# One feed-forward pass with its contraction cut into two halves of 64 rows

## The chip, the cores and the metric

The kernel runs on one core of a Trainium2 chip. The metric is the device time of one execution in microseconds (us); lower is better. Engines are named as the profile names them: PE is the matrix engine's matmuls, PEld its weight loads, DVE, ACT and POOL the vector, scalar and general engines, SP the queue that issues the weight DMAs.

## The reference, cut to what matters

The model has two layers: one of gated linear attention and one of stick-breaking attention, each followed by a feed-forward block. The change touches the second layer's feed-forward block, which computes this for 256 tokens, a width of 2048 and 5632 hidden columns, all in float32:

```python
def swiglu(h, w_gate_up, w_down):
    gate, up = jnp.split(h @ w_gate_up, 2, axis=-1)
    return (jax.nn.silu(gate) * up) @ w_down
...
h = h + swiglu(rmsnorm(h, ffn_norm_w[layer]), ffn_w_gate_up[layer], ffn_w_down[layer])
```

## The kernel before, in words

Every weight is read once from HBM, 512 KB at a time. `load_w` (L111) issues one such DMA on SP, then ACT casts the tile `raw` to a rounded tile `hi` (L119), and DVE subtracts to get the rest, `lo` (L120). Activations are kept in the same two parts, so each product is three matmuls: high by high, high by low, low by high. The pool for `hi` and `lo` has three buffers, that for `raw` four. All of these operands have the type float32r.

`gemm_tok` (L123) makes 512 output columns for both tiles of 128 tokens. The contraction of 2048 runs in 16 steps of 128, two steps to a `load_w`. At each step and for each token tile there are three matmuls (L137), with 128x128 activations loaded into the array and 512 weight columns streamed past; all add into one PSUM tile `acc` for each token tile. So one call issues 16 x 2 x 3 = 96 matmuls, each with its own weight load, and a `load_w` feeds 12 of them. At the end `evac` reads `acc`. There are four `acc` banks, so two calls can follow one another without waiting. Two other PSUM pools hold two banks each: `px`, which the attention stages use, and `tr`, for transposes.

`ffn` (L245) goes through the hidden columns in three passes (`PASSES`, of 4, 4 and 3 blocks of 512). For each block of a pass it calls `gemm_tok` for the gate columns, where `evac_gate` runs Silu on ACT from `acc` into `sg` (L258), and then for the up columns, where `evac_up` multiplies on DVE (L261), transposes four 128x128 pieces for each token tile on PE (L264), and splits the result into `hid_h` (ACT, L267) and `hid_l` (DVE, L268). After its blocks, a pass multiplies the hidden columns with the down weights (`residual_gemm`).

```python
                    gemm_tok(w_gu, KD, lhs, b * NB, evac_gate)
                    gemm_tok(w_gu, KD, lhs, DFF + b * NB, evac_up)
```

The order of instructions on each engine is set by the framework's scheduler from a simulated timeline, not strictly by the order of the program text. [...]

`gemm_col` (L157), used elsewhere, alternates matmuls of 512 columns (L169, L172) and of 256 columns (L170), and `level` (L370) has float32 matmuls of 64 columns behind weight loads of 128 columns (L397).

## Time and profile before

| | us |
|---|---|
| median of two runs | 2282.19 (2281.15 to 2283.24) |
| span of the profiled execution, first to last instruction | 2279.7 |
| PE matmul busy | 2263.7 |
| PE weight load busy | 1891.0 |
| DVE busy | 1238.5 |
| ACT busy | 1046.4 |

The profile is of one execution. A busy time is a union of records, and matmul records overlap: a matmul's record runs until its modelled end, while the next one has already begun. The distance from one start to the next tells how fast matmuls follow one another; the length of one record does not.

### The profile page before, as it was taken

To read this page: it belongs to the slowest core of one execution; us is meant where nothing else is said; L and a number is where in the kernel's file an instruction comes from. 1 tells how busy PE (TensorE), PEld (TensorE's weight loads), DVE (VectorE), ACT (ScalarE), POOL (GpSimd) and SP (SyncE) were. 2 spreads that over 40 slices of the span, in tenths; PEclk is the share of its full clock that TensorE was granted. 3 is DMA by queue.
4 is the path that set the end of the run, shared out by engine and by line. 5 is a ranking of instruction groups with operands and counts; after the bars stand their busy time and mean duration, and the time that the engine had idled before them with its cause. 6 is when DMAs were issued, how large, how long until landed. Compare 5 with 4: busy or idle time off the path is not lost.

```text
span 2279.7 us, 27154 instructions
## 1 busy us (share of the span) xinstructions
PE 2263.7 (99%) x10658; PEld 1891.0 (83%) x10658; DVE 1238.5 (54%) x1251; ACT 1046.4 (46%) x1222; POOL 60.4 (3%) x72
## 2 busy tenths in 40 slices
PE   9999999999999999999999999999999999999998
PEld 7888878888888888888888888888888888888887
DVE  6766455545545545544664567655445444554555
ACT  6544444444434443344554446554444344434444
POOL 2100000000000000000000111000000000000000
PEclk9999999999999999999999999999999999999999
DMA  7554555666666666666566654556666666666664
GB/s 224 169 164 143 153 166 181 188 188 190 188 193 193 189 189 193 194 186 193 185 186 194 186 185 141 167 184 191 186 192 190 193 190 192 186 194 193 191 188 157
DMA packets 242712, 419.23 MB, mean 184 GB/s; under 512 B 12972, under 2 KB 64264, under 8 KB 242456
## 3 DMA queue, kind: packets, MB, share of 16 engines
q1 hardware_dynamic: 242408, 416.44, 60.5%
q8 instruction: 83, 1.36, 0.2%
q10 hardware_dynamic: 176, 1.06, 0.1%
q14 instruction: 45, 0.37, 0.0%
HBM read 415.35 MB, written 2.10 MB: 183 GB/s over the span
## 4 chain that ended last, share of the span: by engine, by line
PE 99%; DVE 0%; issue 0%; DMA 0%; ACT 0%; SPq 0%; POOLq 0%; POOL 0%; DVEq 0%; ACTq 0%
PE acc L137 82%; PE acc L169 7%; PE acc L170 4%; PE px L397 1%; PE tr L264 1%; PE tr L194 1%; PE acc L172 0%; PE acc L154 0%; PE px L494 0%; PE tr L525 0%; PE px L439 0%; DMA raw<-in_gla_w_in_dram 0%; DVE B L356 0%; PE px L409 0%; PE tr L526 0%
## 5 line engine op out<-in xcount | busy, mean ns | idle before, releaser
L120 DVE TENSOR_TENSOR lo<-raw,hi 128x1024 fp32r<-128x1024 f32 (+1 forms) x783 | 972.1, 1243 | 938.4 <-ACT hi L119 937.9
L119 ACT CAST hi<-raw 128x1024 fp32r<-128x1024 f32 (+1 forms) x783 | 823.7, 1052 | 1043.1 <-PE acc L137 904.3
L137 PE MATMUL acc<-hi,xhl 128*128 128x512 f32 x4096 | 1274.7, 391 | 0.8 <-ACT xhl L184 0.8
L137 PEld LDWEIGHTS acc<-hi,xhl 128*128 128x128 f32 x4096 | 769.4, 188 | 161.1 <-issue 1.9
L137 PE MATMUL acc<-lo,xhl 128*128 128x512 f32 x2048 | 799.9, 391 | 0.0
L137 PEld LDWEIGHTS acc<-lo,xhl 128*128 128x128 f32 x2048 | 385.1, 188 | 78.7
L137 PE MATMUL acc<-lo,hid_h 128*128 128x512 f32 x680 | 264.9, 390 | 0.0
L137 PE MATMUL acc<-hi,hid_l 128*128 128x512 f32 x680 | 264.6, 389 | 0.0
L169 PE MATMUL acc<-xhl,hi 128*128 128x512 f32 x735 | 256.1, 396 | 0.6 <-ACT hi L119 0.6
L137 PE MATMUL acc<-hi,hid_h 128*128 128x512 f32 x680 | 240.7, 390 | 0.0
L170 PE MATMUL acc<-xhl,lo 128*128 128x256 f32 x784 | 209.6, 281 | 2.1 <-DVE lo L120 2.0
L169 PEld LDWEIGHTS acc<-xhl,hi 128*128 128x128 f32 x735 | 134.8, 188 | 27.7 <-ACT hi L119 1.0
L170 PEld LDWEIGHTS acc<-xhl,lo 128*128 128x128 f32 x784 | 147.7, 189 | 8.8 <-DVE lo L120 3.0
L137 PEld LDWEIGHTS acc<-hi,hid_l 128*128 128x128 f32 x680 | 127.7, 188 | 26.5
L137 PEld LDWEIGHTS acc<-hi,hid_h 128*128 128x128 f32 x680 | 127.6, 188 | 26.3
L137 PEld LDWEIGHTS acc<-lo,hid_h 128*128 128x128 f32 x680 | 127.6, 188 | 26.1
L184 ACT ACTIVATE xhl<-tr,gains 128x256 fp32r<-128x256 f32 x96 | 40.9, 470 | 28.2 <-PE tr L194 20.9
L185 DVE SCALAR_TENSOR_TENSOR xhl<-tr,gains,xhl 128x256 fp32r<-128x256 f32 x96 | 42.4, 478 | 13.0 <-ACT xhl L184 13.0
L235 DVE TENSOR_TENSOR h<-acc,h 128x512 f32<-128x512 f32 x64 | 41.2, 682 | 7.6 <-PE acc L154 5.2
L258 ACT ACTIVATE sg<-acc,n_r 128x512 f32<-128x512 f32 x44 | 30.0, 690 | 20.8 <-PE acc L137 20.8
L267 ACT CAST hid_h<-tr 128x512 fp32r<-128x512 f32 x44 | 23.6, 589 | 31.4 <-PE tr L264 31.4
L268 DVE TENSOR_TENSOR hid_l<-tr,hid_h 128x512 fp32r<-128x512 f32 x44 | 28.3, 686 | 17.3 <-ACT hid_h L267 17.3
(153 smaller groups left out, 709.1 us busy)
## 6 DMA issues: line engine op xcount, KB each, us to landing
raw<-in_ffn_w_gate_up_dram SPq DMA_DIRECT2D x352, 512.0 KB, 3.9
raw<-in_ffn_w_down_dram SPq DMA_DIRECT2D x176, 512.0 KB, 3.7
raw<-in_gla_w_in_dram SPq DMA_DIRECT2D x97, 512.0 KB, 3.9
raw<-in_sb_w_kv_dram SPq DMA_DIRECT2D x64, 512.0 KB, 3.9
raw<-in_gla_w_out_dram SPq DMA_DIRECT2D x32, 512.0 KB, 3.7
raw<-in_sb_w_q_dram SPq DMA_DIRECT2D x32, 512.0 KB, 3.6
raw<-in_sb_w_out_dram SPq DMA_DIRECT2D x32, 512.0 KB, 3.7
h<-in_x_dram SPq DMA_DIRECT2D x8, 256.0 KB, 5.7
```

Of the source, the lines that this page charges most:

```text
L119: a.copy(hi[:, :n], raw[:, :n])
L120: v.tensor_tensor(lo[:, :n], raw[:, :n], hi.bitcast(F32)[:, :n], ALU.subtract)
L137: pe.matmul(acc[t], l, r[:, j, :], start=(k == 0 and n == 0), stop=(k == kt - 1 and n == 2))
L169: pe.matmul(acc[c], hi[:, j, cs], both, start=first, stop=False)
L170: pe.matmul(acc[c][:, :S], lo[:, j, cs], xhl[:, k0 + j, 0, :], start=False, stop=False)
L184: a.mul(dst_h, src, scale)
L185: v.scalar_tensor_tensor(dst_l, src, scale, dst_h.bitcast(F32), ALU.mult, ALU.subtract)
L194: pe.transpose(tp[:, o : o + P], src(t)[:, j * P : (j + 1) * P], ident)
L235: v.tensor_tensor(hs, acc, hs, ALU.add)
L258: a.activation(sg[t], acc, AF.Silu, scale=r[:, t : t + 1])
L267: a.copy(hh[:, :, ts], tv)
L268: v.tensor_tensor(hl[:, :, ts], tv, hh.bitcast(F32)[:, :, ts], ALU.subtract)
```

## The change

Only the first pass of the second layer's feed-forward block is touched: its four blocks with one gate and one up call each, eight calls. They go to a new function, `gemm_rows`. It loads the same weights in the same way, but each matmul over 128 contraction rows becomes two over 64: rows 0 to 63 of the activations and of the weights at array position (0, 0), and rows 64 to 127 at position (64, 0). The halves of one product are issued one behind the other. The first half adds into a bank of `acc`, the second into a bank of `px`. At the end ACT copies the `px` bank into an SBUF tile, DVE adds the `acc` bank to it, and `evac_gate` or `evac_up` reads that sum from SBUF in place of `acc` from PSUM.

```diff
+    def gemm_rows(w_ap, kt, lhs, c0, evac):
+
+        H = P // 2
+        acc = [(ps_acc.tile([P, NB], F32, name="acc"), ps_x.tile([P, 512], F32, name="px")) for _ in range(NT)]
+        for k0 in range(0, kt, 2):
+            hi, lo = load_w(w_ap, k0, 2, c0, NB)
+            for j in (0, 1):
+                k = k0 + j
+                for t in range(NT):
+                    xh, xl = lhs(k, t)
+                    for n, (l, r) in enumerate(((xh, hi), (xh, lo), (xl, hi))):
+                        for half in (0, 1):
+                            rs = slice(half * H, (half + 1) * H)
+                            pe.matmul(acc[t][half], l[rs], r[rs, j, :], start=(k == 0 and n == 0), stop=(k == kt - 1 and n == 2), tile_position=(half * H, 0))
+        for t in range(NT):
+            both = stat.tile([P, NB], F32, name="junk")
+            a.copy(both, acc[t][1])
+            v.tensor_tensor(both, acc[t][0], both, ALU.add)
+            evac(t, both)
...
-                    gemm_tok(w_gu, KD, lhs, b * NB, evac_gate)
-                    gemm_tok(w_gu, KD, lhs, DFF + b * NB, evac_up)
+                    gemm = gemm_rows if layer and blocks is PASSES[0] else gemm_tok
+                    gemm(w_gu, KD, lhs, b * NB, evac_gate)
+                    gemm(w_gu, KD, lhs, DFF + b * NB, evac_up)
```

The rest of the diff takes comments and docstrings out.

## Rows read from the trace of the kernel before

**Rows 1.** The page: the span, busy time by engine (part 1), the granted TensorE clock in 40 slices (part 2, tenths of full speed) and the chain of work that ended last, by engine and by line (part 4).

```profile
span 2279.7 us, 27154 instructions
...
PE 2263.7 (99%) x10658; PEld 1891.0 (83%) x10658; DVE 1238.5 (54%) x1251; ACT 1046.4 (46%) x1222; POOL 60.4 (3%) x72
...
PEclk9999999999999999999999999999999999999999
...
PE 99%; DVE 0%; issue 0%; DMA 0%; ACT 0%; SPq 0%; POOLq 0%; POOL 0%; DVEq 0%; ACTq 0%
PE acc L137 82%; PE acc L169 7%; PE acc L170 4%; PE px L397 1%; PE tr L264 1%; PE tr L194 1%; PE acc L172 0%; PE acc L154 0%; PE px L494 0%; PE tr L525 0%; PE px L439 0%; DMA raw<-in_gla_w_in_dram 0%; DVE B L356 0%; PE px L409 0%; PE tr L526 0%
```

**Rows 2.** Busy time of each engine in stretches of the pass that the change touches, then the granted clock, the DMA engines' share and GB/s: the whole pass's gate and up calls, and the second of its four blocks.

```profile
1542.60:1720.40 177.80, 177.80 (x802) 147.52 (x801) 89.42 (x86) 79.72 (x88) 0.69 (x1) 1.00 0.64 189
...
1587.00:1631.40 44.40, 44.40 (x201) 36.86 (x200) 22.19 (x21) 19.19 (x21) 0.00 (x0) 1.00 0.64 188
```

**Rows 3.** Groups of PE instructions between 1543 and 1721 us: line, operation, output and inputs, shapes, count, busy time, mean ns of one record, idle time before.

```profile
L137 PE MATMUL acc<-hi,xhl 128*128 128x512 f32 x510 | 158.2, 390 | 0.0
L137 PE MATMUL acc<-lo,xhl 128*128 128x512 f32 x256 | 99.7, 390 | 0.0
L264 PE MATMUL tr<-ident,sg 128*128 128x128 f32 x24 | 3.1, 272 | 0.0
```

**Rows 4.** Timeline of PE in the pass, one `load_w` long: start, duration, line, tiles, count merged into the row. Twelve matmuls start from the first row up to the last, the last not counted.

```profile
1709.59 0.39 PE L137 MATMUL acc<-lo,xhl 128*128 128x512 f32 x1
1709.82 0.39 PE L137 MATMUL acc<-hi,xhl 128*128 128x512 f32 x1
1710.04 0.39 PE L137 MATMUL acc<-lo,xhl 128*128 128x512 f32 x1
...
1711.63 0.84 PE L137 MATMUL acc<-hi,xhl 128*128 128x512 f32 x3
1712.31 0.39 PE L137 MATMUL acc<-lo,xhl 128*128 128x512 f32 x1
```

**Rows 5.** Timeline of PEld, the weight loads, at the beginning of the same stretch.

```profile
1709.59 0.19 PEld L137 LDWEIGHTS acc<-hi,xhl 128*128 128x128 f32 x1
1709.82 0.19 PEld L137 LDWEIGHTS acc<-lo,xhl 128*128 128x128 f32 x1
```

**Rows 6.** Timeline of PE in a `gemm_col`, where matmuls of 512 and of 256 columns alternate, each behind a weight load of 128 columns.

```profile
1301.07 0.28 PE L170 MATMUL acc<-xhl,lo 128*128 128x256 f32 x1
1301.19 0.39 PE L169 MATMUL acc<-xhl,hi 128*128 128x512 f32 x1
1301.42 0.28 PE L170 MATMUL acc<-xhl,lo 128*128 128x256 f32 x1
1301.54 0.39 PE L169 MATMUL acc<-xhl,hi 128*128 128x512 f32 x1
...
1303.15 0.28 PE L170 MATMUL acc<-xhl,lo 128*128 128x256 f32 x1
```

**Rows 7.** From the line's own view, the weight loads and matmuls of L397 (count, min/median/max ns); then, from a timeline, a run of 32 of those matmuls of 64 columns.

```profile
L397 PEld LDWEIGHTS px<-lev x224: 187/192/192, 147.8 to 230.0; 128*128 128x128 f32 x112
L397 PE MATMUL px<-lev x224: 217/275/275, 147.9 to 230.1; 128*128 128x64 f32 x112
...
147.91 3.68 PE L397 MATMUL px<-lev 128*128 128x64 f32 x32
```

**Rows 8.** Timelines of ACT and PE around the end of the second block's gate call; a bracket is idle time before and what ended it.

```profile
1606.91 1.05 ACT L119 CAST hi<-raw 128x1024 fp32r<-128x1024 f32 x1 [1.67 <-PE acc L137]
1608.95 1.37 ACT L258 ACTIVATE sg<-acc,n_r 128x512 f32<-128x512 f32 x2 [0.98 <-PE acc L137]
1610.22 1.04 ACT L119 CAST hi<-raw 128x1024 fp32r<-128x1024 f32 x1
1612.35 1.05 ACT L119 CAST hi<-raw 128x1024 fp32r<-128x1024 f32 x1 [1.09 <-PE acc L137]
...
1608.52 0.62 PE L137 MATMUL acc<-hi,xhl 128*128 128x512 f32 x2
1608.98 0.39 PE L137 MATMUL acc<-lo,xhl 128*128 128x512 f32 x1
1609.20 0.84 PE L137 MATMUL acc<-hi,xhl 128*128 128x512 f32 x3
```

**Rows 9.** Timelines of DVE and PE around the end of the second block's up call.

```profile
1630.90 1.40 DVE L261 SCALAR_TENSOR_TENSOR sg<-acc,n_r,sg 128x512 f32<-128x512 f32 x2
1632.48 1.23 DVE L120 TENSOR_TENSOR lo<-raw,hi 128x1024 fp32r<-128x1024 f32 x1 [0.17 <-ACT hi L119]
...
1635.95 1.03 PE L264 MATMUL tr<-ident,sg 128*128 128x128 f32 x8
```

**Rows 10.** Groups of ACT and DVE instructions: the pass's Silu, the down projection's addition into the residual stream, and the casts and subtractions of weights with the idle time before them.

```profile
L258 ACT ACTIVATE sg<-acc,n_r 128x512 f32<-128x512 f32 x8 | 5.4, 689 | 3.0 <-PE acc L137 3.0
L119 ACT CAST hi<-raw 128x1024 fp32r<-128x1024 f32 x65 | 68.4, 1054 | 89.7 <-PE acc L137 88.1 <-ACT xhl L184 1.0 <-ACT junk L202 0.5
L235 DVE TENSOR_TENSOR h<-acc,h 128x512 f32<-128x512 f32 x1 | 0.7, 680 | 0.0
L120 DVE TENSOR_TENSOR lo<-raw,hi 128x1024 fp32r<-128x1024 f32 x64 | 78.3, 1225 | 85.0 <-ACT hi L119 85.0
```

## The prediction

> **What bounds the kernel now.** I read the page first, from the top. [...] The stretches come next, for the place of the change: the touched pass runs from 1542.6 to 1720.4 us, PE is busy through all of it at clock 1.00, while DVE and ACT work half of the time (22.2 and 19.2 us of a block's 44.4) and the DMA engines two thirds [rows 2]. The groups of this stretch hold 766 matmuls of line 137 in the window, and by the code it is 8 calls x 96 = 768 [rows 3].

> Then the timeline, for the speed of PE. Twelve matmuls take 1709.59 to 1712.31, 2.72 us, so one starts 0.2267 us behind the other, though each record lasts 0.39 [rows 4]. The reader is to see two more things. A record outlives the next one's start by 0.39 - 0.227 = 0.16 us, so a matmul leaves the array while the next enters. And the load for the next matmul starts together with the running matmul (1709.59 and 1709.82 stand in both views) and is over after 0.19 us [rows 4, 5], so new weights go into rows that are still at work. At 0.2267 us each, 768 matmuls are 174.1 us, 7.6% of the span: the whole stake.

> **The change part by part.**

> *The matmuls.* 768 products become 1536, and a half still streams all 512 columns. Nothing in the trace runs on part of the array's rows beside other work, so the cost of a pair of halves is bounded. One end is that they run side by side. Then a pair can't be faster than its two weight loads, which keep 128 columns each. The load's rate is seen where matmuls are short: 32 matmuls of 64 columns behind a load each take 3.68 us, so (3.68 - 0.275) / 31 = 0.110 us for one load with its matmul [rows 7]. Two make 0.220, just below 0.2267. A second reading is `gemm_col`: six rounds of a 256 and a 512 column matmul take 1301.07 to 1303.15, 0.3467 each, and less 0.2267 that leaves 0.120 for the short one [rows 6], so two make 0.240. The same rows say that the engine can start a load and a matmul every 0.110 us, so double the number of instructions is not a limit of its own. The other end is that the second half waits until the first is through: 0.453 a pair.

> I take the near end, in the middle of 0.220 and 0.240, 0.230: 768 x (0.230 - 0.2267) = +2.5 us, with -5.1 and +10.2 as bounds of this case. The reason is what rows 4 and 5 show: the array is not held as a whole by one matmul, since it takes new weights during it and lets the next in before its end, and the halves share neither rows nor a PSUM bank. No row shows two at once, which is why the other end keeps a large chance.

> *The px banks.* A call takes both banks of `px`, and the next call needs them at once; `acc` has four. In rows 8, ACT reads the first token tile's result at 1608.95. The second tile's three matmuls follow, and the next call begins at 1609.20 + 0.227 = 1609.43. Now ACT has to copy that `px` bank first: 0.69 us as the Silu over the same 128x512 [rows 10], to 1609.64, and the first matmul of a second half can start at about 1609.68. That is 0.25 us late. The second bank is copied by 1610.33, when PE wants it at 1609.68 + 0.68 = 1610.36: no further loss. But if the order on ACT puts the first Silu ahead of the second copy, that copy waits for DVE's addition (0.68, rows 10) and the Silu (0.69), 1.4 us more; a weight cast in that place costs 1.05 [rows 8]. So 0.25 to 1.6 us at each of seven seams, 1.8 to 11.2 us. I take 0.7, nearer the low end because in rows 8 and 9 ACT and DVE serve the ending call before the weights of the next: +4.9 us.

> *Copies and additions.* 16 copies on ACT (11.0 us) and 16 additions on DVE (10.9 us) are new. At a call's end ACT waits 0.98 us for PE [rows 8], and for all weight casts together it waits 88.1 us in this stretch, DVE 85.0 for casts [rows 10]. The cast behind the Silus would move from 1610.22 by 1.4 us to 1611.6, and with its subtraction (1.05 + 1.23) be ready at 1613.9; its weights come two `load_w` (5.44 us) after 1609.43, at 1614.87. So nothing is added; with this 1 us of cover gone, each of the eight ends would cost up to 1.4 us.

> *The transposes.* `sg` of an up call is ready at 1630.90 + 1.40 = 1632.30, the transposes stand at 1635.95 in PE's order [rows 9]: 3.6 us of slack for a chain that gets 1.4 us longer for each token tile. Zero, and up to 4 x 1.4 = 5.6 us if the scheduler puts them earlier.

> *Switches.* The pass enters and leaves the split array once, and each of four up calls has transposes over the full array, in at most two groups: 18 changes. The trace has none. If the array has to be empty at one, it costs the tail that now overlaps, 0.16 us [rows 4], so 0 to 2.9 us, and I take 1.5.

> The DMAs, their number and their queue stay; at 0.64 of the DMA engines [rows 2] a pass a little longer asks less of them.

> Sum: 2279.7 + 2.5 + 4.9 + 1.5 = 2288.6 us of span. The median of the runs is 2.5 us above the profiled span, which makes 2291. Bounds of this case: -5.1 + 1.8 = -3.3 and 10.2 + 11.2 + 5.6 + 2.9 = +29.9, so 2279 to 2312.

> **The rivals.**

> *Turns, not side by side (the change doesn't do what it says).* A matmul holds PE until its 512 columns are in, whichever rows it uses. Each half then costs the 0.2267 us of a whole one, so +174.1 us. The copies fit under the slower seams, the switches stay: 2279.7 + 174.1 + 1.5 + 2.5 = 2458, slower by 7.7%. For it: every matmul of the trace starts only when the one before has streamed [rows 4, 6], and no row shows otherwise. Against it: the overlap of loads and tails. It decides the verdict from a price of (45.6 - 6.4) / 768 = 0.051 us above today's, a pair of 0.278, where 45.6 us is the 2% that a measurement of this kernel can tell from no change.

> *A half's load waits for its own half.* The halves overlap, but new weights for a group of rows only go in when that group has finished, as they would if there were no second place for them. A pair then takes a load and a matmul, 0.110 + 0.2267 = 0.337, and the sum is 768 x 0.110 = +84.5, with 3.5 for seams and switches 2370. Against it: the load that begins with the running matmul in rows 4 and 5. [...]

> *A gain.* If splitting hides the 0.2267 - 0.220 that separates today's pace from the loads, -5.1 us is the most, 0.2%: inside "same". A pair of 0.167, needed for 2%, lies below two loads.

> *Order at the seams.* The upper bounds of seams and transposes come together: 2279.7 + 2.5 + 11.2 + 5.6 + 1.5 + 2.5 = 2303, still "same".

> **How the numbers follow.** Side by side, with good or bad seams, gets 0.57; turns 0.30; loads that wait 0.12; something faster than all of this 0.01. The likeliest is side by side at 2291, and its own range is 2279 to 2312. Without the turns less than 8 in 10 would be held, so the range goes from 2277 up to 2466, turns with bad seams. Faster by over 2% 0.01, within 2% 0.57, slower 0.42.

> **What would show it.** In the changed profile, the timeline of line 137's successor should show two starts close together or 0.115 us apart, and a pair every 0.22 to 0.24 us; turns show starts 0.227 apart throughout and a pass of about 350 us instead of 177.8; waiting loads show PEld records that begin behind matmul ends, and pairs of 0.337. A seam shows as a stretch without matmul starts at a call's end, with PE released by the copy on ACT; late transposes show as PE idle released by DVE `sg`. The forecast is wrong if a pair costs over 0.278, or if seams cost more than 1.6 us each.

## The result, and the profile after

The changed kernel takes 2301.97 us (2301.02 to 2302.92, two runs) against 2282.19: a ratio of 1.0087, interval 1.0058 to 1.0117. It is slower by 19.8 us and within 2%, 11 us above the 2291 that was forecast and inside both stated ranges, 2279 to 2312 and 2277 to 2466. The profiled span grew from 2279.7 to 2299.1 us.

The page of the changed kernel: span, busy time by engine, and the chain that ended last, by line; they answer to [rows 1].

```profile
span 2299.1 us, 28730 instructions
...
PE 2283.2 (99%) x11426; PEld 1909.2 (83%) x11426; DVE 1249.7 (54%) x1267; ACT 1054.9 (46%) x1238; POOL 60.7 (3%) x72
...
PE acc L137 73%; PE acc L189 7%; PE px L155 5%; PE acc L190 4%; PE acc L155 3%; PE px L418 1%; PE tr L284 1%; PE tr L214 1%; PE acc L192 0%; PE acc L174 0%; PE px L515 0%; PE tr L546 0%; PE px L460 0%; DMA raw<-in_gla_w_in_dram 0%; DVE B L377 0%
```

PE has 768 matmuls more (11426 for 10658) and is still 99% busy, so this page alone can't tell work from waste: two matmuls at a time count once, and one that runs alone on half the rows counts as much. The halves are line 155. The stretches of the pass, columns as in [rows 2]: all of its gate and up calls, and one block from its transposes to the next block's.

```profile
1542.20:1739.30 197.10, 197.10 (x1569) 165.44 (x1568) 99.11 (x98) 88.02 (x102) 0.70 (x1) 1.00 0.59 172
1594.70:1644.30 49.60, 49.60 (x394) 41.88 (x393) 25.19 (x25) 21.39 (x24) 0.00 (x0) 1.00 0.60 170
```

The pass takes 197.1 in place of 177.8 us, so 19.3 of the 19.4 us by which the span grew are here; the clock stays at 1.00. A block takes 49.6 for 44.4. Now PE's timeline early in the pass, where [rows 4] had single matmuls, and under it the weight loads, where [rows 5] had one.

```profile
1543.07 0.39 PE L155 MATMUL acc<-hi,xhl 64*128 64x512 f32 x1
1543.08 0.39 PE L155 MATMUL px<-hi,xhl 64*128 64x512 f32 x1
1543.31 0.38 PE L155 MATMUL acc<-lo,xhl 64*128 64x512 f32 x1
1543.31 0.38 PE L155 MATMUL px<-lo,xhl 64*128 64x512 f32 x1
1543.53 0.39 PE L155 MATMUL acc<-hi,xhl 64*128 64x512 f32 x1
1543.54 0.39 PE L155 MATMUL px<-hi,xhl 64*128 64x512 f32 x1
```

```profile
1543.08 0.18 PEld L155 LDWEIGHTS acc<-lo,xhl 64*128 64x128 f32 x1
1543.08 0.18 PEld L155 LDWEIGHTS px<-lo,xhl 64*128 64x128 f32 x1
```

The halves do run side by side: they start within 0.01 us of each other, a pair every 0.23 us (1543.08, 1543.31, 1543.54), and their loads start together too (both at 1543.08). Pairs are not where the time went. This is PE's timeline around the end of the second block's gate call:

```profile
1615.97 0.39 PE L155 MATMUL px<-hi,xhl 64*128 64x512 f32 x1
1615.98 0.61 PE L155 MATMUL acc<-hi,xhl 64*128 64x512 f32 x2
...
1618.02 0.61 PE L155 MATMUL acc<-hi,xhl 64*128 64x512 f32 x2
1618.26 0.49 PE L155 MATMUL px<-hi,xhl 64*128 64x512 f32 x1
...
1618.93 0.39 PE L155 MATMUL acc<-hi,xhl 64*128 64x512 f32 x1
...
1620.90 0.61 PE L155 MATMUL px<-hi,xhl 64*128 64x512 f32 x2
1621.13 0.50 PE L155 MATMUL acc<-lo,xhl 64*128 64x512 f32 x1
```

From 1615.97 to 1618.26 only first halves (`acc`) start, one every 0.227 us; from 1618.93 to 1621.13 only second halves (`px`). Each side stands still once, the second halves for 2.29 us and the first for 2.20, where 0.227 is normal. The engine that frees the bank had long been done, as ACT's timeline there shows:

```profile
1615.71 1.26 ACT L158 COPY junk<-px 128x512 f32<-128x512 f32 x2 [0.99 <-PE px L155]
```

The first `px` bank was copied by about 1616.3 and the second by 1616.97, yet the next call's first second half starts 1.3 us after that. The reason stands in PE's list as it was compiled. Written as runs, with A a first half, B a second half, (n) n pairs AB, and t a transpose, a block of the pass reads:

```
(80) 15xA (1) 15xB (80) 15xA (1) 7xB 4xt 2xB 4xt 6xB
```

A seam is the join of two of the eight calls. At each of the seven, 16 first halves (15xA and the A of the pair behind them) stand ahead of 16 second halves (that pair's B and 15 more, with transposes among them where an up call ended). In program order they alternate; it is the scheduler that moved them, and the first experiment shows that it does so only where the second bank is still held.

### The profile page after: what moved, and what is told of

It reads as the page before. It is cut to its first block, busy times and chain, and to the rows that moved or that the text cites. A ratio compares the mean times of both kernels' runs of the same rounds, so it can differ in the third digit from the quotient of the medians.

```text
span 2299.1 us, 28730 instructions
## 1 busy us (share of the span) xinstructions
PE 2283.2 (99%) x11426; PEld 1909.2 (83%) x11426; DVE 1249.7 (54%) x1267; ACT 1054.9 (46%) x1238; POOL 60.7 (3%) x72
## 4 chain that ended last, share of the span: by engine, by line
PE 99%; issue 0%; DVE 0%; DMA 0%; ACT 0%; SPq 0%; POOLq 0%; POOL 0%; DVEq 0%; ACTq 0%
PE acc L137 73%; PE acc L189 7%; PE px L155 5%; PE acc L190 4%; PE acc L155 3%; PE px L418 1%; PE tr L284 1%; PE tr L214 1%; PE acc L192 0%; PE acc L174 0%; PE px L515 0%; PE tr L546 0%; PE px L460 0%; DMA raw<-in_gla_w_in_dram 0%; DVE B L377 0%
## 5 line engine op out<-in xcount | busy, mean ns | idle before, releaser
L137 PE MATMUL acc<-hi,xhl 128*128 128x512 f32 x3584 | 1115.3, 391 | 1.3 <-ACT xhl L204 1.3
L137 PEld LDWEIGHTS acc<-hi,xhl 128*128 128x128 f32 x3584 | 672.9, 188 | 141.5 <-issue 1.9
L137 PE MATMUL acc<-lo,xhl 128*128 128x512 f32 x1792 | 699.6, 391 | 0.0
L137 PEld LDWEIGHTS acc<-lo,xhl 128*128 128x128 f32 x1792 | 336.8, 188 | 69.0
L155 PE MATMUL px<-hi,xhl 64*128 64x512 f32 x512 | 159.8, 389 | 0.0
L155 PE MATMUL acc<-hi,xhl 64*128 64x512 f32 x512 | 157.8, 388 | 0.0
L155 PEld LDWEIGHTS px<-hi,xhl 64*128 64x128 f32 x512 | 93.8, 184 | 13.7 <-issue 0.5
L155 PE MATMUL acc<-lo,xhl 64*128 64x512 f32 x256 | 99.9, 390 | 0.0
L155 PE MATMUL px<-lo,xhl 64*128 64x512 f32 x256 | 99.3, 388 | 0.0
L155 PEld LDWEIGHTS acc<-hi,xhl 64*128 64x128 f32 x512 | 94.0, 184 | 5.1 <-issue 0.5
```

Of the source, the lines that this page charges most:

```text
L137: pe.matmul(acc[t], l, r[:, j, :], start=(k == 0 and n == 0), stop=(k == kt - 1 and n == 2))
L155: pe.matmul(acc[t][half], l[rs], r[rs, j, :], start=(k == 0 and n == 0), stop=(k == kt - 1 and n == 2), tile_position=(half * H, 0))
```

## The experiments

Seven kernels were run, in two groups, the later ones chosen on what the first had shown. Ratios are to the kernel before on the same chip.

**Other banks.** Gate calls keep `px`, up calls take the transposes' banks, which are free at that time, so no bank is needed while the call before still holds it.

```diff
-        acc = [(ps_acc.tile([P, NB], F32, name="acc"), ps_x.tile([P, 512], F32, name="px")) for _ in range(NT)]
+        second = second or (lambda: ps_x.tile([P, 512], F32, name="px"))
+        acc = [(ps_acc.tile([P, NB], F32, name="acc"), second()) for _ in range(NT)]
...
+                    in_tr = {"second": lambda: ps_tr.tile([P, 512], F32, name="tr")} if gemm is gemm_rows else {}
-                    gemm(w_gu, KD, lhs, DFF + b * NB, evac_up)
+                    gemm(w_gu, KD, lhs, DFF + b * NB, evac_up, **in_tr)
```

> The up calls take their second banks from the pool of the transposes instead of px, so no call waits for a bank that the call before it still holds; in PE's list first and second halves then alternate through the whole pass, where the changed kernel has seven seams with 16 first halves ahead of 16 second halves. Theory A (the order at the seams costs the time): each seam's loss of 2.09 us (a gap of 2204 ns between two first halves where 227 is normal, and a late second start of 339 for 227) goes, 7 x 2.09 = 14.6, so 2302 - 14.6 = 2287 us. Theory B (a pair costs more than a whole matmul, or the changes between split and whole array cost it): no more than 2 us are won, about 2300.

Measured: 2285.29 us, ratio 1.0017 (1.0008 to 1.0026), 16.7 us less than the changed kernel. Theory A holds and B falls. In PE's list of this run the halves alternate through all seven seams. The pass in the stretches' view, and PE's timeline across a seam:

```profile
1541.90:1722.80 180.90, 180.90 (x1569) 147.02 (x1568) 98.28 (x98) 87.42 (x102) 0.69 (x1) 1.00 0.60 187
```

```profile
1608.74 0.39 PE L156 MATMUL acc<-hi,xhl 64*128 64x512 f32 x1
1608.74 0.39 PE L156 MATMUL px<-hi,xhl 64*128 64x512 f32 x1
...
1610.55 0.39 PE L156 MATMUL acc<-hi,xhl 64*128 64x512 f32 x1
1610.56 0.39 PE L156 MATMUL px<-hi,xhl 64*128 64x512 f32 x1
1610.78 0.39 PE L156 MATMUL acc<-hi,xhl 64*128 64x512 f32 x1
1610.78 0.39 PE L156 MATMUL tr<-hi,xhl 64*128 64x512 f32 x1
...
1611.46 0.39 PE L156 MATMUL acc<-hi,xhl 64*128 64x512 f32 x1
1611.46 0.39 PE L156 MATMUL tr<-hi,xhl 64*128 64x512 f32 x1
```

The call changes from `px` to `tr` at 1610.78 without a break, and twelve pairs take 1608.74 to 1611.46, 2.72 us: to the hundredth what twelve whole matmuls took in [rows 4]. A pair costs 0.2267 us, the price of one. The pass takes 180.9 us where the changed kernel takes 197.1, so 16.2 us of the pass go with the seams, 2.3 each. At each seam the standing still seen above (2.20 us for 0.227) and the late start behind it (0.34 for 0.227) are 2.1 of that.

**Order pinned.** The banks stay as in the change; each matmul of a call is held behind the one before it in the program's order.

```diff
-                            pe.matmul(acc[t][half], l[rs], r[rs, j, :], start=(k == 0 and n == 0), stop=(k == kt - 1 and n == 2), tile_position=(half * H, 0))
+                            m = pe.matmul(acc[t][half], l[rs], r[rs, j, :], start=(k == 0 and n == 0), stop=(k == kt - 1 and n == 2), tile_position=(half * H, 0))
+                            if (k, t, n, half) != (0, 0, 0, 0):
+                                tc.keep_in_program_order(m)
```

> The banks stay as in the changed kernel, but every matmul of a call is pinned behind the one before it in the program's order, so halves alternate and PE has to wait for the copy of px at a seam. Theory A (order): the list is as in the run with other banks, and what is left at a seam is the wait itself, 0.25 us where the copies come first and up to 0.7: 2287 + 7 x 0.25 to 0.7 = 2289 to 2292 us, with short stretches at the seams in which PE starts nothing. Rival (the wait for the bank costs the time and the order only shows it): the seams keep their 2.1 us, 2302.

Measured: 2288.28 us, ratio 1.0026 (1.0017 to 1.0035). So it is the order and not the wait for the bank: with the wait kept, 13.7 of the 16.7 us are back. PE's timeline at the end of the first block's up call, and PEld's behind it:

```profile
1589.51 0.39 PE L155 MATMUL px<-hi,xhl 64*128 64x512 f32 x1
1589.52 0.39 PE L155 MATMUL acc<-hi,xhl 64*128 64x512 f32 x1
1589.89 0.50 PE L155 MATMUL px<-hi,xhl 64*128 64x512 f32 x1
1589.89 0.50 PE L155 MATMUL acc<-lo,xhl 64*128 64x512 f32 x1
1590.23 0.39 PE L155 MATMUL px<-lo,xhl 64*128 64x512 f32 x1
```

```profile
1589.89 0.18 PEld L155 LDWEIGHTS px<-hi,xhl 64*128 64x128 f32 x1 [0.41 <-ACT junk L160]
1590.00 0.19 PEld L155 LDWEIGHTS px<-lo,xhl 64*128 64x128 f32 x1
```

PE waits here for ACT's copy of the `px` bank (line 160 of this run). The wait is 0.38 for 0.227 us, and the pair behind it comes 0.34 later; its loads begin 0.11 us behind the late ones (1590.00 after 1589.89). That is 0.27 us a seam by this view, (2288.28 - 2285.29) / 7 = 0.43 by the totals.

**Same rows.** Both halves work on rows 0 to 63; rows 64 to 127 are left out.

```diff
-                            rs = slice(half * H, (half + 1) * H)
+                            rs = slice(0, H)
-                            pe.matmul(acc[t][half], l[rs], r[rs, j, :], start=(k == 0 and n == 0), stop=(k == kt - 1 and n == 2), tile_position=(half * H, 0))
+                            pe.matmul(acc[t][half], l[rs], r[rs, j, :], start=(k == 0 and n == 0), stop=(k == kt - 1 and n == 2), tile_position=(0, 0))
```

> Both halves use rows 0 to 63 of the operands and of the array, each still with its own bank; rows 64 to 127 of the contraction are left out. The order of the instructions is that of the changed kernel. If separate rows are what lets halves run side by side, halves now take turns, 0.2267 us each: + 768 x 0.2267 = 174.1, and the seams' 14.6 us is no extra loss any more, so 2302 + 159.5 = 2461 us, with starts 0.227 apart. If separate banks or two instructions in flight are enough, it stays at 2302 with starts close together.

Measured: 2460.24 us, one run. Its PE timeline:

```profile
1560.36 0.39 PE L155 MATMUL acc<-hi,xhl 64*128 64x512 f32 x1
1560.58 0.39 PE L155 MATMUL px<-hi,xhl 64*128 64x512 f32 x1
```

The halves take turns, 0.227 us apart (six steps from 1559.90 to 1561.26), though their banks differ. Separate rows, of the operands and of the array together, make the difference (2460.24 for 2301.97), and this is the price that the rival of turns would have had: 2458 was worked out for it.

**Half width.** Other banks, and from the second contraction step on each half streams 256 columns; the rest is left out.

```diff
+                            w = NB if k == 0 else NB // 2
-                            pe.matmul(acc[t][half], l[rs], r[rs, j, :], start=(k == 0 and n == 0), stop=(k == kt - 1 and n == 2), tile_position=(half * H, 0))
+                            pe.matmul(acc[t][half][:, :w], l[rs], r[rs, j, :w], start=(k == 0 and n == 0), stop=(k == kt - 1 and n == 2), tile_position=(half * H, 0))
...
```

> As the run with other banks, but from the second contraction step on each half streams 256 of its 512 columns; the rest of the columns is left out. It asks whether the two weight loads of a pair run side by side. If they do, a pair can start every 0.120 us, the pace of a single matmul of 256 columns, wherever weights are at hand, and the supply of weights sets the total: somewhere from 2205 to 2275 us. If loads follow one another, as the prediction's lower bound of 0.220 has it, pairs start every 0.22 us or more and the total is about 2287 - 768 x 0.007 = 2280 or above.

Measured: 2232.61 us, one run. Its timelines of PE and of PEld, where weights were at hand:

```profile
1552.10 0.28 PE L157 MATMUL acc<-hi,xhl 64*128 64x256 f32 x1
1552.10 0.28 PE L157 MATMUL px<-hi,xhl 64*128 64x256 f32 x1
1552.22 0.28 PE L157 MATMUL acc<-hi,xhl 64*128 64x256 f32 x1
1552.22 0.28 PE L157 MATMUL px<-hi,xhl 64*128 64x256 f32 x1
```

```profile
1552.10 0.19 PEld L157 LDWEIGHTS acc<-hi,xhl 64*128 64x128 f32 x1
1552.10 0.19 PEld L157 LDWEIGHTS px<-hi,xhl 64*128 64x128 f32 x1
```

A pair every 0.12 us (1552.10, 1552.22) with two loads in it, both recorded from 1552.10 for 0.19 us: in this run the loads for rows 0 to 63 and for rows 64 to 127 go side by side. Two in a row would take 0.220, by the estimate that the prediction makes from [rows 7].

**Alternate.** Other banks and order pinned, but of the two contraction steps of a `load_w` only the first is split.

```diff
+                        if j:
+                            tc.keep_in_program_order(pe.matmul(acc[t][0], l, r[:, j, :], start=False, stop=(k == kt - 1 and n == 2)))
+                            continue
                         for half in (0, 1):
...
```

> Banks as in the first run and the order pinned, but only every other contraction step is split; the steps between are whole matmuls over 128 rows that add into the first bank. So PE changes from split to whole and back once in each of 64 load_w. Theory (what is left above the kernel before, about 3.3 us, is the change between split and whole array): a change there and back costs about 0.35 us, read from the run with other banks (316 for 231 ns into a transpose, 202 for 28 ns out of it, 334 for 227 ns to the second split start), so 2282 + 64 x 0.35 = about 2304 us. Rival (what is left are the copies and additions at the ends of calls, or pairs that are a little slow): no more than 2286.

Measured: 2312.82 us, ratio 1.0134 (1.0117 to 1.0151), more than was expected. PE's timeline through one change each way (whole matmuls are L155, halves L159), and PEld's at the first of them:

```profile
1602.38 0.40 PE L155 MATMUL acc<-hi,xhl 128*128 128x512 f32 x1
1602.71 0.50 PE L159 MATMUL acc<-hi,xhl 64*128 64x512 f32 x1
...
1603.05 0.39 PE L159 MATMUL acc<-lo,xhl 64*128 64x512 f32 x1
...
1603.98 0.39 PE L159 MATMUL acc<-hi,xhl 64*128 64x512 f32 x1
1604.30 0.51 PE L155 MATMUL acc<-hi,xhl 128*128 128x512 f32 x1
1604.64 0.40 PE L155 MATMUL acc<-lo,xhl 128*128 128x512 f32 x1
```

```profile
1602.15 0.19 PEld L155 LDWEIGHTS acc<-hi,xhl 128*128 128x128 f32 x1
1602.71 0.18 PEld L159 LDWEIGHTS acc<-hi,xhl 64*128 64x128 f32 x1 [0.37 <-issue]
1602.82 0.19 PEld L159 LDWEIGHTS acc<-lo,xhl 64*128 64x128 f32 x1
```

Across a change the next start comes 0.32 to 0.33 us later instead of 0.227, and the one after that 0.34: the first load begins only with its matmul (both at 1602.71), and the second 0.11 us behind it (1602.82). That is 0.21 us a change and 0.43 there and back. By the trace this run changes there and back 69 times (64 in the contraction, five at transposes), and the run with other banks nine times (three blocks' transposes twice, those at the pass's beginning twice, and the pass itself); the totals give (2312.82 - 2285.29) / (69 - 9) = 0.46. The rival, by which copies, additions or slow pairs make the rest and this run stays at 2286, falls. For the run with other banks, 9 x 0.35 to 0.46 = 3.2 to 4.1 us, and it lies 3.3 above the kernel before (1.8 to 5.9 by its interval): little is left for anything else.

**Runs of 6 and of 12.** Other banks and order pinned, with the loop over halves moved outward: outside the token tiles, so that six first halves stand ahead of six second ones, or outside both contraction steps, twelve ahead of twelve.

```diff
-                for t in range(NT):
-                    xh, xl = lhs(k, t)
-                    for n, (l, r) in enumerate(((xh, hi), (xh, lo), (xl, hi))):
-                        for half in (0, 1):
+                for half in (0, 1):
+                    for t in range(NT):
+                        xh, xl = lhs(k, t)
+                        for n, (l, r) in enumerate(((xh, hi), (xh, lo), (xl, hi))):
...
```

> Banks as in the first run, order pinned, but not in turns: the six first halves of a contraction step (two token tiles by three products) stand ahead of its six second halves. Theory (in the changed kernel a second half started while three first halves ahead of it had not: a list of 16 and 16 left each side alone for about 10 slots, not 16, so the engine passes a few waiting matmuls of one row group into a queue of their own, one running and three behind it): runs of 6 keep both row groups fed, and the time is that of the first run, about 2285 us. Rival (matmuls start strictly in their order): 6 pairs take 11 slots in place of 6, 128 x 5 x 0.2267 = +145 us, 2430.

> The same with runs of 12, all first halves of a load_w ahead of its second halves. Theory of the queue of three: the second half's run begins 8 slots after the first half's run, and the next first half's run 8 slots after that, so 12 pairs take 16 slots in place of 12: 64 x 4 x 0.2267 = +58 us, about 2343. Rival (strict order): 12 pairs take 22 or more slots, + 145 us, 2430. Rival (the engine looks so far ahead that runs do not matter): 2285.

Measured: 2286.53 us for runs of 6, ratio 1.0020 (1.0010 to 1.0029), and 2361.96 us, one run, for runs of 12. Strict order is refuted by both (2430 was due), a lookahead without bound by the second (2285). The queue of three, an estimate from the changed kernel's starts, fits the first; the second is 19 us above its 2343. PE's timeline with runs of 12, from the last first half of one run to the first of the next:

```profile
1601.94 0.49 PE L156 MATMUL tr<-hi,xhl 64*128 64x512 f32 x1
...
1602.62 0.39 PE L156 MATMUL acc<-hi,xhl 64*128 64x512 f32 x1
...
1603.89 0.49 PE L156 MATMUL acc<-hi,xhl 64*128 64x512 f32 x1
...
1605.85 0.49 PE L156 MATMUL tr<-hi,xhl 64*128 64x512 f32 x1
```

The first of twelve second halves (`tr`) starts at 1601.94, ahead of three first halves that stand before it in the list (the last one at 1602.62). The next run of second halves starts at 1605.85, 3.91 us on. The estimate of three gives 16 slots, 3.63 us. Of the other 0.28 us, 0.21 is that a side that had stood still makes its second start 0.33 us behind its first in place of 0.227, once on each side in the 3.91 (1601.94 to 1602.27 for `tr`, 1603.89 to 1604.22 for `acc`). 64 x (3.91 - 2.72) = 76 us, and 2285.29 + 76 = 2361.

## Why the prediction was right or wrong

**The verdict and the case were right, the number partly by luck.** Side by side was the likeliest, and the run on the same rows shows by contrast what turns would have cost. But the change cost 19.8 us where the sum had 8.9. The 2302 lies inside 2279 to 2312 only because the top of that range also held 10.2 us for slow pairs and 5.6 for transposes, which cost nothing, while the seams went beyond their own bound of 11.2. That the rival on order at the seams has 2303 is chance: it adds waits of PE for banks and late transposes, and neither made the time. By the prediction's own sign the seams came out wrong, with more than 1.6 us each.

**The pair** was taken at 0.230 us (+2.5 us); it measures 0.2267, +0. The bounds of 0.220 and 0.240 rested on two loads that follow one another. They don't: in the half-width run a pair with both its loads starts every 0.12 us, so that bound was no bound. The margin was too small to matter at 512 columns.

**The px banks are the step that failed**, in mechanism and so in size. The text put 0.25 to 1.6 us on each of seven seams and took 0.7, in all 4.9 us. The change pays 2301.97 - 2285.29 = 16.7, 2.4 a seam (2.3 by the stretches). Nor is a seam a stretch without starts, as was foretold: PE goes on starting halves every 0.227 us, but for 2.29 us on one side alone, and then for 2.20 on the other. The wait that was priced exists and measures 0.27 to 0.43, near the low end. What was left out is that the scheduler answers an occupied bank by reordering: the worst case considered was an ACT instruction in the wrong place, not 16 matmuls of one row group ahead of their partners on PE itself. What such a reordering costs on whole matmuls no run shows; with halves, each one that runs alone takes the 0.227 us in which a pair could have run.

**Switches** were given 1.5 us, 0 to 2.9. About 3.3 are left for them in the run with other banks. The count of 18 came out, by two errors that cancel (the fourth block's transposes fall behind the pass, those of the residual stream at its beginning inside), the price did not: the tail of 0.16 us was the author's estimate of a change, and the runs show 0.21 to 0.23, with the load behind a change beginning only with its matmul (1602.71 in the alternate run).

**Copies, additions and transposes** were put at nothing, and little is left for them: by the timelines the seams are 16.2 us and 18 changes at 0.21 are 3.8, together 20.0 where 19.8 was measured. With other banks the twelve pairs across a seam keep their pace, 2.72 us, though ACT begins its copies inside them:

```profile
1610.30 1.27 ACT L159 COPY junk<-px 128x512 f32<-128x512 f32 x2 [0.99 <-PE px L156]
```

**The two rivals that named another price for a pair** (0.453 and 0.337) fell, as a pair takes 0.2267. Nor does a half's load wait for its own half: in the rows of 1543.08 a half's next weights are loaded from within 0.01 us of that half's own start (1543.07), for 0.18 us, and its successor starts at 1543.31, not 0.337 on.

The forecast of 2291 thus had +2.5, +4.9 and +1.5 where 0, 16.7 and 3.3 were measured.

No version that does all of the work beats the kernel before; the run with half width is shorter because it leaves columns out. Nothing suggests that one would: a pair does the work of one whole matmul in the same 0.2267 us.

## What to carry to other kernels

Cutting a full contraction into two row groups gained nothing here even at best, since a pair costs one whole matmul (0.2267 us at 512 columns, 0.12 at 256); what it adds are more banks, more evacuation and about 0.21 us for each change between split and whole work. Where row groups are used for contractions that are short anyway, look at the compiled order: here runs of 6 cost 1.2 us in the whole pass and runs of 12 77 us, and a bank that came free late made the scheduler pull partners apart by 16, which cost 2.3 us a seam where the wait itself costs 0.27 to 0.43. Give the banks to calls so that none is needed while the call before still holds it (2285.29 us for 2301.97), or pin the order (2288.28).

## What was not expected of the hardware

In the half-width run two weight loads of 128 columns for separate rows take the time of one: both are recorded from 1552.10 for 0.19 us, as one is in [rows 5], and a pair starts every 0.12 us, as the single short matmul in [rows 6]. Behind a matmul whose rows had stood still (1601.94 with runs of 12), or one behind a change of the split (1602.71 in the alternate run), the next start came 0.33 to 0.34 us on, 0.11 late.
